# Score rectangles copied by ScalarE at block sizes 128 and 64 instead of masked copies by VectorE

## The chip, the cores and the metric

The kernel runs on one core of a Trainium2 chip. The metric is the device time of one execution in microseconds. A kernel's time is the median of several executions.

## The reference

One inference step of a two-layer decoder: 512 prompt tokens and 64 sample tokens (eight sequences of eight), width 1024. Each layer projects the normalised tokens, runs four recurrent mixers (HGRN2, GLA, RWKV-7, retention), merges them through gates, and ends with a SwiGLU feed-forward part. The change lies in the mixer core that HGRN2 and GLA share. Its scores decay with the distance of the two tokens:

```python
b = jnp.cumsum(gb, axis=2)
diff = b[:, :, :, None, :] - b[:, :, None, :, :]
decay = jnp.exp(jnp.where(causal > 0, diff, 0.0)) * causal
scores = jnp.sum(qb[:, :, :, None, :] * kb[:, :, None, :, :] * decay, axis=-1)
o = (jnp.einsum('bhts,bhsv->bhtv', scores, vb)
     + jnp.einsum('bhtk,bhkv->bhtv', qb * jnp.exp(b), S))
```

A score counts only when its key token is not later than its query token. The diagonal (a token with itself) has decay 1.

## The kernel before

`gla_core` works on chunks of 128 tokens, four for the prompt, and one of 64 for the samples. It runs once for HGRN2 (`nt` = 2, two tiles of channels) and once for GLA (`nt` = 1) in each layer, so there are 16 prompt chunks in all. Scores of a chunk are made level by level: at level m (64, 32, 16, 8, 4, 2, 1) the chunk is cut into blocks of 2m tokens, and the keys of a block's first half meet the queries of its second half. `gla_level` prepares a level: VectorE subtracts the decay sum at the middle of the block (L1107, tile `le`), ScalarE takes two exponentials of it (L1110), VectorE (HGRN2) or GpSimd (GLA) makes the scaled keys `lk` (L1111), and VectorE the scaled queries `qt` or `qg` (L1122, L1115). TensorE then multiplies them (L1026, tile `lvp` in PSUM), and `gla_pred` puts the wanted part of that product into the score tile `sc` by one `copy_predicated` on VectorE with an integer mask `lev` (L1137). The mask of a level also takes the diagonal score of each block's first query token (position m of the block). The diagonal positions that no level takes, one in 128 prompt tokens and one in 8 sample tokens, stand in a short list: `gd0` (GpSimd, L980 and L981) holds q times k there, a matmul sums it over a head's channels (`gdp`, L986 and L988), VectorE multiplies by v (`gdv`, L992 and L993) and adds it to the outputs at the end (L1092 and L1093).

The loop over levels prepares level i+1, then calls `gla_pred` for level i-1, then yields, then issues the matmul of level i. The `lvp` tiles and most other PSUM tiles of the mixers share a ring of two buffers (`g`). The masks, `sc` and the padded query tiles are allocated once.

The mixers are Python generators that are advanced between the projection units (`mix`, L1623), by a table of start and due positions (`PACE`). A projection unit is a matmul series (`pb<-h,whl`, L241 to L243) whose weights come by DMA into `raw`, are split into two float16 parts by ScalarE (L228) and VectorE (L229), and whose result ScalarE moves out of PSUM (L487 and others). The tile framework then orders the instructions of each engine itself, starting from the order of the text. Each engine runs its own list in order.

Other work that matters below: the RWKV mixer's VectorE and ScalarE parts (lines 577 to 965), and `head_rms_out` (L515 and L516, tile `hsq`), whose logarithm and exponential each come with a load of ScalarE's function table.

Of the kernel before, what the change touches and what calls it, by code (L numbers as in the profile page):

```python
# [16 lines left out]
ADD, SUB, MUL, MAX, MIN = ALU.add, ALU.subtract, ALU.mult, ALU.max, ALU.min  # L17

D = 1024
SEQ = 512  # L20
NS = 64
T = SEQ + NS
# [152 lines left out]
class Net:  # L175
# [792 lines left out]
    def gla_core(self, l, q, k, v, lg, nt, load, result):  # L968
# [3 lines left out]
        nc = self.nc  # L972
        hpt = 4 // nt
        dk = 128 // hpt
        B = lg
        d0 = self.t("gq", [128, nt, 12], "gd0")
        for j in range(nt):
            self.chunk_sums(B[:, j], lg[:, j], "ones")

            nc.gpsimd.tensor_tensor(d0[:, j, 0:4], q[:, j, 0:SEQ:128], k[:, j, 0:SEQ:128], op=MUL)  # L980
            nc.gpsimd.tensor_tensor(d0[:, j, 4:12], q[:, j, SEQ:T:8], k[:, j, SEQ:T:8], op=MUL)  # L981
            yield
        dp = self.psum("g", [128, 2, 12], "gdp")
        for j in range(2):
            if nt == 2:
                nc.tensor.matmul(dp[:, j], self.cf("head"), d0[:, j], start=True, stop=True)  # L986
            else:
                nc.tensor.matmul(dp[:, j], self.cf("gla_head")[:, 128 * j:128 * j + 128], d0[:, 0],  # L988
                                 start=True, stop=True)
        dv = self.t("gq", [128, 2, 12], "gdv")  # L990
        for j in range(2):
            nc.vector.tensor_tensor(dv[:, j, 0:4], dp[:, j, 0:4], v[j][:, 0:SEQ:128], op=MUL)  # L992
            nc.vector.tensor_tensor(dv[:, j, 4:12], dp[:, j, 4:12], v[j][:, SEQ:T:8], op=MUL)  # L993
        O = [self.t("gs", [128, T], "gl_o") for _ in range(2)]
        vw = 256 // nt
        S = None
        for c in range(5):
            samp = c == 4
            n = 64 if samp else 128
            ts = slice(128 * c, 128 * c + n)  # L1000
            if samp:
                sst = load(0)
                sc = self.scs
            else:
                sc = self.sc[self.nsc % 2]
# [3 lines left out]
            if nt == 1:  # L1009

                qm = self.qm[c % 2][:, :, :n]
                for h in range(4):
                    r = slice(32 * h, 32 * h + 32)
# [3 lines left out]
            for i, (li, m) in enumerate(lv):  # L1017
# [6 lines left out]
                ps = self.psum("g", [128, 4, 64], f"lvp{nt}")  # L1024
# [15 lines left out]
            if samp:  # L1040
                qz = self.padded(nt)
                for h in range(hpt):
                    r = slice(dk * h, dk * h + dk)
# [45 lines left out]
        if nt == 1:  # L1089
            nc.sync.dma_start(out=self.io["sample_gla"][l].rearrange("b h k v -> (h k) b v"), in_=so)  # L1090
        for j in range(2):
            nc.vector.tensor_tensor(O[j][:, 0:SEQ:128], O[j][:, 0:SEQ:128], dv[:, j, 0:4], op=ADD)  # L1092
            nc.vector.tensor_tensor(O[j][:, SEQ:T:8], O[j][:, SEQ:T:8], dv[:, j, 4:12], op=ADD)  # L1093
        result += [O, S]
        yield

# [35 lines left out]

    def gla_pred(self, sc, ps, li, m, n):

        so = sc[:n, :, :n].rearrange("p h (b u i) -> p h b u i", u=2, i=m)[:, :, :, 1]
        mk = self.lev[:n, li, None, :n // 2].to_broadcast([n, 4, n // 2])
        self.nc.vector.copy_predicated(so, mk.rearrange("p h (b i) -> p h b i", i=m),  # L1137
                                       ps[:n, :, :n // 2].rearrange("p h (b i) -> p h b i", i=m))
# [815 lines left out]
```

## Time and profile before

| | us |
|---|---|
| median of 3 runs (2200.36 to 2207.76) | 2204.15 |
| the profiled execution, its own time | 2207.72 |
| its span from the first to the last instruction | 2205.9 |
| TensorE busy with matmuls | 2039.1 |
| VectorE busy | 1636.6 |
| ScalarE busy | 1081.3 |
| GpSimd busy | 682.3 |

PE is TensorE's matmuls, PEld its weight loads, DVE VectorE, ACT ScalarE, POOL GpSimd. A busy TensorE isn't TensorE at its peak, since matmuls overlap and their ends are modelled. The mixers of the first layer lie between about 56 and 420 us, those of the second about 1080 us later. HGRN2's prompt chunks are worked on from 68 to 175 us, GLA's from 180 to 325 us.

### The profile page before, as it was taken

The numbers are of one execution on the slowest core, as the hardware profiler recorded it, in microseconds if no ns is written. First come the engines' busy times: TensorE is split into PE (matmuls) and PEld (weight loads), VectorE is DVE, ScalarE is ACT, GpSimd is POOL, SyncE is SP. The second block draws the span as 40 slices with busy tenths as digits, with TensorE's granted clock in tenths as the row PEclk, the third lists the DMA queues.
The fourth block names the chain that finished last, engine by engine and source line by source line (L and its number), as shares of the span: only waits on it lengthen the run. The fifth ranks groups of instructions, "written<-read, shape, count | busy, mean of one in ns | idle before, by whom it ended". The sixth has DMA issues, their size and how long they took to land.

```text
span 2205.9 us, 42236 instructions
## 1 busy us (share of the span) xinstructions
PE 2039.1 (92%) x15754; PEld 1612.3 (73%) x15754; DVE 1636.6 (74%) x3409; ACT 1081.3 (49%) x2524; POOL 682.3 (31%) x889
## 2 busy tenths in 40 slices
PE   7989999998888899999999889989998988999998
PEld 5767787786676677777777778768776766777776
DVE  7889667768785899863488986586788779998441
ACT  6554546345444555442466355453645465554332
POOL 2223222146550544320012142213465316443000
PEclk9999999999999999999999999999999999999999
DMA  6312224333435344343421222242343443443331
GB/s 181 84 41 62 58 58 110 77 83 92 116 98 177 80 116 120 87 135 103 122 68 46 58 62 60 73 111 62 87 120 88 131 141 97 111 116 87 121 106 51
DMA packets 373498, 209.59 MB, mean 95 GB/s; under 512 B 59810, under 2 KB 360410, under 8 KB 373292
## 3 DMA queue, kind: packets, MB, share of 16 engines
q1 hardware_dynamic: 365516, 192.73, 31.6%
q0 software_dynamic: 7776, 14.16, 3.6%
q8 instruction: 124, 2.03, 0.4%
q14 instruction: 82, 0.67, 0.1%
HBM read 173.72 MB, written 16.59 MB: 86 GB/s over the span
## 4 chain that ended last, share of the span: by engine, by line
PE 47%; DVE 28%; ACT 8%; issue 7%; DMA 5%; POOL 3%; SPq 1%; DVEq 0%; ACTq 0%; POOLq 0%
PE pb L243 5%; PE pb L242 5%; PE pb L241 5%; PE xb L243 4%; PE xb L242 4%; PE xb L241 4%; DVE hA L1704 4%; DVE hS L1704 3%; DVE sc L1745 2%; DVE fy L1776 2%; DVE whl L229 2%; DVE su L1745 2%; PE fsS L1731 2%; PE fsS L1729 2%; PE fsS L1730 2%
## 5 line engine op out<-in xcount | busy, mean ns | idle before, releaser
L241 PE MATMUL pb<-h,whl 128*128 128x288 f16 (+1 forms) x1504 | 435.8, 290 | 4.4 <-ACT h L464 2.2
L243 PE MATMUL pb<-h,whl 128*128 128x288 f16 (+1 forms) x1504 | 435.5, 290 | 3.2 <-DVE whl L229 3.1
L242 PE MATMUL pb<-h,whl 128*128 128x288 f16 (+1 forms) x1504 | 436.0, 290 | 0.6 <-DVE h L465 0.4
L229 DVE SCALAR_TENSOR_TENSOR whl<-raw,whl 128x512 f16<-128x512 f32 (+1 forms) x352 | 253.8, 730 | 134.3 <-ACT whl L228 132.2
L242 PEld LDWEIGHTS <-whl 128*128 128x128 f16 (+1 forms) x2784 | 275.4, 99 | 88.0 <-issue 13.5
L243 PEld LDWEIGHTS <-whl 128*128 128x128 f16 (+1 forms) x2784 | 275.1, 99 | 88.0 <-issue 12.7
L241 PEld LDWEIGHTS <-whl 128*128 128x128 f16 (+1 forms) x2784 | 277.2, 100 | 76.6 <-issue 3.6
L228 ACT ACTIVATE whl<-raw 128x512 f16<-128x512 f32 (+1 forms) x352 | 213.3, 618 | 168.2 <-PE pb L243 51.9
L243 PE MATMUL xb<-fa,whl 128*128 128x288 f16 x704 | 201.3, 286 | 0.0
L242 PE MATMUL xb<-fa,whl 128*128 128x288 f16 x704 | 201.3, 286 | 0.0
L241 PE MATMUL xb<-fa,whl 128*128 128x288 f16 x704 | 201.3, 286 | 0.0
L1729 PE MATMUL fsA<-h,hA 128*128 128x288 f16 x432 | 124.3, 288 | 14.9 <-DVE gu L1550 10.8
L1729 PE MATMUL fsS<-st,hS 128*128 128x288 f16 x456 | 132.6, 291 | 5.9 <-ACT hS L1703 5.9
L1731 PE MATMUL fsS<-st,hS 128*128 128x288 f16 x456 | 132.4, 290 | 0.4 <-DVE hS L1704 0.3
L1730 PE MATMUL fsS<-st,hS 128*128 128x288 f16 x456 | 132.5, 291 | 0.0
L1731 PE MATMUL fsA<-h,hA 128*128 128x288 f16 x432 | 124.2, 288 | 1.7 <-DVE hA L1704 1.6
L1730 PE MATMUL fsA<-h,hA 128*128 128x288 f16 x432 | 124.3, 288 | 0.0
L1707 POOL TENSOR_TENSOR raw<-raw 128x512 f32<-128x512 f32 x52 | 79.0, 1520 | 134.2 <-DVE hA L1704 129.7
L1729 PEld LDWEIGHTS <-hS 128*128 128x128 f16 x864 | 85.7, 99 | 35.9 <-ACT hS L1703 13.7
L1704 DVE SCALAR_TENSOR_TENSOR hA<-sraw,hA 128x512 f16<-128x512 f32 x110 | 103.1, 945 | 10.6 <-ACT hA L1703 10.6
L1707 POOL TENSOR_TENSOR sraw<-sraw 128x512 f32<-128x512 f32 x60 | 89.7, 1499 | 51.4 <-DVE hA L1704 45.7
L1731 PEld LDWEIGHTS <-hS 128*128 128x128 f16 x864 | 85.7, 99 | 24.8 <-DVE hS L1704 2.6
(486 smaller groups left out, 5257.8 us busy)
## 6 DMA issues: line engine op xcount, KB each, us to landing
raw<-in_w_in SPq DMA_DIRECT2D x208, 256.0 KB
sraw<-in_w_ffn_in SPq DMA_DIRECT2D x40, 512.0 KB
raw<-in_w_ffn_out SPq DMA_DIRECT2D x80, 256.0 KB
raw<-in_w_ffn_in SPq DMA_DIRECT2D x78, 256.0 KB
x<-xd SPq DMA_DIRECT2D x32, 288.0 KB
raw<-sraw POOLq DMA_DIRECT2D x34, 256.0 KB, 3.3
sraw<-in_w_in SPq DMA_DIRECT2D x32, 256.0 KB
raw<-in_w_out SPq DMA_DIRECT2D x32, 256.0 KB
```

The source lines that it names most:

```text
L228: nc.scalar.activation(hl[:, 0, :n], raw[:, :n], AF.Copy, scale=WS)
L229: nc.vector.scalar_tensor_tensor(hl[:, 1, :n], raw[:, :n], WS, hl[:, 0, :n], op0=MUL, op1=SUB)
L241: nc.tensor.matmul(ps, wh, hi, start=i == 0, stop=False)
L242: nc.tensor.matmul(ps, wh, lo, start=False, stop=False)
L243: nc.tensor.matmul(ps, wl, hi, start=False, stop=i == len(ks) - 1)
L1704: nc.vector.scalar_tensor_tensor(hl[:, 1], a, WS, hl[:, 0], op0=MUL, op1=SUB)
L1707: nc.gpsimd.tensor_tensor(dst, a, b, op=op)
L1729: nc.tensor.matmul(ps, w[a][:, 0, k], hi, start=k == 0, stop=False)
L1730: nc.tensor.matmul(ps, w[a][:, 0, k], lo, start=False, stop=False)
L1731: nc.tensor.matmul(ps, w[a][:, 1, k], hi, start=False, stop=k == 3)
L1745: nc.vector.tensor_tensor(o, a, p, op=ADD)
L1776: nc.vector.scalar_tensor_tensor(y, u, PH * AS, sg, op0=MUL, op1=MUL)
```

## The change

The two coarsest levels of a prompt chunk (m = 64 and m = 32) no longer use the mask. For each block, ScalarE copies the rectangle of keys of the first half by queries of the second half from PSUM to `sc`: one copy of 64 partitions by 4 heads by 64 columns at m = 64, and two copies of 32 partitions by 4 heads by 32 columns at m = 32. The rectangle has no diagonal element, so the list of diagonal scores takes every 32nd prompt token in place of every 128th: 16 prompt entries and 8 sample entries instead of 4 and 8. Levels 16 to 1 and the sample chunk stay as they are.

```diff
-        d0 = self.t("gq", [128, nt, 12], "gd0")
+        d0 = self.t("gq", [128, nt, 24], "gd0")
...
-            nc.gpsimd.tensor_tensor(d0[:, j, 0:4], q[:, j, 0:SEQ:128], k[:, j, 0:SEQ:128], op=MUL)
-            nc.gpsimd.tensor_tensor(d0[:, j, 4:12], q[:, j, SEQ:T:8], k[:, j, SEQ:T:8], op=MUL)
+            nc.gpsimd.tensor_tensor(d0[:, j, 0:16], q[:, j, 0:SEQ:32], k[:, j, 0:SEQ:32], op=MUL)
+            nc.gpsimd.tensor_tensor(d0[:, j, 16:24], q[:, j, SEQ:T:8], k[:, j, SEQ:T:8], op=MUL)
...
-        dp = self.psum("g", [128, 2, 12], "gdp")
+        dp = self.psum("g", [128, 2, 24], "gdp")
...
-        dv = self.t("gq", [128, 2, 12], "gdv")
+        dv = self.t("gq", [128, 2, 24], "gdv")
         for j in range(2):
-            nc.vector.tensor_tensor(dv[:, j, 0:4], dp[:, j, 0:4], v[j][:, 0:SEQ:128], op=MUL)
-            nc.vector.tensor_tensor(dv[:, j, 4:12], dp[:, j, 4:12], v[j][:, SEQ:T:8], op=MUL)
+            nc.vector.tensor_tensor(dv[:, j, 0:16], dp[:, j, 0:16], v[j][:, 0:SEQ:32], op=MUL)
+            nc.vector.tensor_tensor(dv[:, j, 16:24], dp[:, j, 16:24], v[j][:, SEQ:T:8], op=MUL)
...
-            nc.vector.tensor_tensor(O[j][:, 0:SEQ:128], O[j][:, 0:SEQ:128], dv[:, j, 0:4], op=ADD)
-            nc.vector.tensor_tensor(O[j][:, SEQ:T:8], O[j][:, SEQ:T:8], dv[:, j, 4:12], op=ADD)
+            nc.vector.tensor_tensor(O[j][:, 0:SEQ:32], O[j][:, 0:SEQ:32], dv[:, j, 0:16], op=ADD)
+            nc.vector.tensor_tensor(O[j][:, SEQ:T:8], O[j][:, SEQ:T:8], dv[:, j, 16:24], op=ADD)
...
     def gla_pred(self, sc, ps, li, m, n):
 
+        if m >= 32:
+            for b in range(n // (2 * m)):
+                r = slice(2 * m * b, 2 * m * b + m)
+                self.nc.scalar.copy(sc[r, :, r.stop:r.stop + m], ps[r, :, m * b:m * b + m])
+            return
```

## Rows read from the trace of the kernel before

**Rows 1.** The page's first part: busy us, share of the span, instructions.
```profile
PE 2039.1 (92%) x15754; PEld 1612.3 (73%) x15754; DVE 1636.6 (74%) x3409; ACT 1081.3 (49%) x2524; POOL 682.3 (31%) x889
```

**Rows 2.** The page's chain that ended last, shares by engine.
```profile
PE 47%; DVE 28%; ACT 8%; issue 7%; DMA 5%; POOL 3%; SPq 1%; DVEq 0%; ACTq 0%; POOLq 0%
```

**Rows 3.** Busy time by stretch: stretch, length, PE, PEld, DVE, ACT, POOL, clock, DMA.
```profile
110.00:165.00 55.00, 47.24 (x334) 37.00 (x333) 48.62 (x114) 29.68 (x72) 12.05 (x20) 0.91 0.16 40
165.00:215.00 50.00, 46.59 (x350) 36.52 (x349) 45.80 (x141) 21.16 (x72) 17.90 (x35) 1.00 0.27 65
...
260.00:345.00 85.00, 84.07 (x666) 69.43 (x664) 51.88 (x146) 35.96 (x119) 23.12 (x50) 1.00 0.23 61
```

**Rows 4.** TensorE's timeline: start, length; in brackets the idle time before, and releaser.
```profile
102.75 0.68 PE L1026 MATMUL lvp<-qt,lk 128*128 128x128 f32 x4 [0.48 <-DVE qt L1122]
133.41 1.19 PE L1026 MATMUL lvp<-qt,lk 128*128 128x128 f32 x4 [3.50 <-DVE qt L1122]
...
184.56 0.42 PE L1026 MATMUL lvp<-qt,lk 128*64 128x64 f32 x4 [0.36 <-DVE qt L1122]
190.73 0.42 PE L1026 MATMUL lvp<-qt,lk 128*64 128x64 f32 x4 [0.58 <-DVE qt L1122]
...
225.41 1.19 PE L1026 MATMUL lvp<-qg,lk 128*128 128x256 f32 x2 [2.64 <-ACT hsq L515]
...
1304.98 0.67 PE L1026 MATMUL lvp<-qg,lk 128*128 128x256 f32 x2 [2.64 <-ACT hsq L515]
```

**Rows 5.** The masked copies of line 1137: durations in ns, and their waits.
```profile
L1137 DVE COPY_PREDICATED sc<-lev,lvp x112: 416/435/739, 69.2 to 1393.5; 128x256 f32<-128x256 int32 x112
...
  PE lvp L1026: 13.2, 19
```

**Rows 6.** VectorE's timeline around masked copies of the two coarse levels.
```profile
93.59 0.43 DVE L1137 COPY_PREDICATED sc<-lev,lvp 128x256 f32<-128x256 int32 x1
93.92 0.68 DVE L577 TENSOR_TENSOR rw_r<-cur 128x511 f32<-128x511 f32 x1
...
128.71 0.44 DVE L1137 COPY_PREDICATED sc<-lev,lvp 128x256 f32<-128x256 int32 x1
...
132.15 0.51 DVE L1111 TENSOR_TENSOR lk<-hg_k,le 128x256 f32<-128x256 f32 x1
...
182.84 0.43 DVE L1137 COPY_PREDICATED sc<-lev,lvp 128x256 f32<-128x256 int32 x1
...
186.17 0.43 DVE L1137 COPY_PREDICATED sc<-lev,lvp 128x256 f32<-128x256 int32 x1
```

**Rows 7.** ScalarE's copies out of PSUM into tile gkh, by form, durations in ns.
```profile
L1155 ACT COPY gkh<-gtp x24: 266/372/373, 84.9 to 1519.0; 128x256 f32<-128x256 f32 x16, 128x128 f32<-128x128 f32 x8
...
L1165 ACT COPY gkh<-gtp x8: 256/258/263, 196.8 to 1533.5; 64x128 f32<-64x128 f32 x8
```

**Rows 8.** ScalarE's timeline in HGRN2's third chunk.
```profile
117.85 1.28 ACT L1110 ACT_TABLE_LOAD   x1
119.14 0.31 ACT L1110 ACTIVATE le<-le 128x128 f32<-128x128 f32 x1
119.36 0.67 ACT L695 ACTIVATE rn<-rn 128x576 f32<-128x576 f32 x1
119.93 0.29 ACT L1110 ACTIVATE le<-le 128x128 f32<-128x128 f32 x1
...
131.27 0.51 ACT L1110 ACTIVATE le<-le 128x128 f32<-128x128 f32 x2
```

**Rows 9.** Busy time and granted clock behind three of TensorE's waits (columns as above).
```profile
133.50:137.00 3.50, 3.50 (x17) 2.59 (x18) 3.46 (x10) 1.45 (x6) 0.38 (x1) 0.55 0.47 122
225.40:229.00 3.60, 3.60 (x14) 2.34 (x15) 1.61 (x3) 3.10 (x6) 0.34 (x1) 0.53 0.24 54
1305.00:1309.00 4.00, 4.00 (x32) 3.35 (x33) 2.04 (x4) 3.36 (x7) 0.77 (x1) 1.00 0.23 52
```

**Rows 10.** GpSimd's products of the diagonal list in GLA, durations in ns.
```profile
L980 POOL TENSOR_TENSOR gd<-gl_q,gl_k x2: 259/259/259, 170.7 to 1250.2; 128x4 f32<-128x4 f32 x2
```

## The prediction

> **What bounds the kernel now.** I read the page's busy shares first: TensorE 92%, VectorE 74%, ScalarE 49% [rows 1]. By these alone VectorE would be cover for everything. The chain of waits says otherwise: 28% of it is VectorE and 8% ScalarE [rows 2]. So the next question is where VectorE sets the pace, and that a table by stretch answers. From 110 to 165 us VectorE is busy 48.62 of 55 us and TensorE 47.24; from 165 to 215 us VectorE is busy 45.80 of 50. From 260 to 345 us, where most of GLA's chunks run, TensorE is busy 84.07 of 85 us and VectorE 51.88 [rows 3]. So the same masked copy can be worth something in HGRN2's part and nothing in GLA's.
>
> What a shorter VectorE list can give back is only time in which TensorE stands still behind VectorE. TensorE's timeline gives these waits one by one. Those behind `qt` that bear on the change are 0.48 us at 102.75, 3.50 at 133.41, 0.36 at 184.56 and 0.58 at 190.73; one of 2.64 at 225.41 stands behind ScalarE's `hsq`. The second layer repeats the pattern about 1080 us later: the same 2.64 at 1304.98 [rows 4]. I therefore work out one layer and double it.
>
> **What is removed.** 16 prompt chunks with two coarse levels each lose 32 of the 112 full-size masked copies [rows 5]. Their length is bimodal: median 435 ns, longest 739 [rows 5]; the five coarser levels stand at 0.43 in the timeline, as at 93.59 and 128.71 [rows 6], so 32 x 0.435 = 13.9 us of VectorE's busy time go. On VectorE's list each takes less than its length, since the next instruction starts before it ends: 93.59 to 93.92 is 0.33 us [rows 6]. I use 0.33 for what a removed copy gives back where VectorE is the bound. A copy that itself waited for TensorE gives nothing; masked copies waited 19 times, 13.2 us in all [rows 5].
>
> Place by place, in the first layer:
>
> HGRN2, first chunk: TensorE has no wait behind it. 0.
>
> HGRN2, second chunk: the copy at 93.59 has a full VectorE list behind it up to the `qt` that releases TensorE at 102.75. Of the 0.48 us there, 0.33 go: -0.33 [rows 4, 6].
>
> HGRN2, third chunk: the copy at 128.71 stands ahead of the 3.50 us wait, in a VectorE stretch without gaps [rows 4, 6]. It looks like the best place, but `lk` at 132.15 also needs the two exponentials that begin at 131.27 and take 0.51, thus end at 131.78 [rows 6, 8]. That is 0.37 us of slack on ScalarE. The two new copies of m = 32 come ahead of these exponentials and take about 0.32 together (2 x 0.258 less the overlaps, below), so ScalarE's slack is used up just as VectorE would come 0.33 earlier. I take 0; the ends are -0.33 (the copies are placed behind) and +0.32 (they also delay the function table's load before it).
>
> HGRN2, fourth chunk: its two copies are among those that waited for TensorE [rows 5]. 0; a full VectorE list there would make it -0.66.
>
> GLA, first chunk: it runs while HGRN2's sample chunk keeps VectorE full (45.80 of 50 us [rows 3]). Its copies at 182.84 and 186.17 precede the `qt` of 184.56 and 190.73, with waits of 0.36 and 0.58: -0.33 each [rows 4, 6].
>
> GLA, second chunk: here the change costs. The wait of 2.64 us at 225.41 stands behind a stretch of ScalarE with its table loads [rows 4]. The copy of m = 64 now joins that list.
>
> GLA, third and fourth chunk: TensorE has 0.93 us idle in 85 [rows 3]; VectorE's gain and ScalarE's cost are both covered by matmuls. 0. If TensorE were not the bound there, these 4 copies would give 1.3 us per layer.
>
> **What is added.** Per chunk one ScalarE copy of 64 x 256 and two of 32 x 128. No row has these partitions, but 64 x 128 took 258 ns and 128 x 256 372 [rows 7], so I price by columns: 0.372 + 2 x 0.258 = 0.888 us, times 16 is 14.2 us of ScalarE. ScalarE's list also overlaps: an exponential of 0.31 begins at 119.14 and the next instruction at 119.36 [rows 8], 0.09 before its end. So the m = 64 copy costs the list 0.28 and each m = 32 copy 0.17. In the second GLA chunk this is +0.28 on TensorE's wait. Bounds for one copy: 0, since ScalarE is idle half the time [rows 1], and its full length.
>
> A copy now waits on ScalarE for its matmul, in place of the masked copy on VectorE. Queued behind it are the exponentials of later levels, the weight splits and the PSUM moves of the projections, and VectorE's `lk` and TensorE's next series wait for these. `gla_pred` runs one step after its matmul was issued, so mostly the product is there.
>
> The list of diagonals grows from 12 to 24 columns. On GpSimd the 128 x 4 product took 259 ns [rows 10]; at most four times that for 16 entries, 1.04 us, six times: 6 x 0.78 = 4.7 us at most, on an engine busy 12.05 of 55 us [rows 3], and read only a matmul series later. On TensorE and VectorE it is 12 more elements in instructions whose price is nearly all start-up. 0; without GpSimd's idle time it would be those 4.7 us.
>
> **Sum.** Per layer -0.33 - 0.33 - 0.33 + 0.28 = -0.71, both layers -1.4 us. The profiled execution's own time is 2207.72 (span 2205.9 and 1.8 around it), so it would become 2206.3. Against the median of the runs, 2204.15, it is 2202.7. The bounds of the parts, if everything lay on the path: -13.9 (2190.2) and +14.2 (2218.4).
>
> **A clock that follows the waits.** Behind the 3.50 us wait the granted clock was 0.55 for 3.5 us, mostly the 1.2 GHz level; behind the 2.64 us wait it was 0.53 in the first layer and 1.00 in the second [rows 9]. A drop costs about (1 - 0.55) x 3.5 = 1.6 or (1 - 0.53) x 3.6 = 1.7 us. So 0.3 us on a wait near this length can cost or save 1.7 more, once per place. The Trainium skill (TensorE: Matmul & The Clock Gate, "HAM oscillation") says that TensorE's clock is halved behind long idle stretches, so such a wait is paid twice. These rows agree in one layer and not in the other. By that rule the drop would come in both layers when the 2.64 grows, and the sum would be 2204.4. I give a second drop at this place a quarter of the first case's chance below, 0.13; it stays inside that case's own range.
>
> **Rivals.** (a) Faster: VectorE's list is the real bound wherever HGRN2 is active, and its lateness is carried from wait to wait. Then the eight copies of HGRN2 and the two of GLA's first chunk count with their whole length: 20 x 0.435 = 8.7 us, 2195.5. For it: VectorE busy 48.62 of 55 and 45.80 of 50 [rows 3]. Against it: several of these copies waited for TensorE themselves, so VectorE was early there. The Trainium skill (Perfetto Trace Analysis, "Optimizing Scalar/DVE Operations") says that work may be moved to ScalarE where VectorE is saturated; the rows show it nearly saturated in these two stretches alone.
>
> (b) Slower: ScalarE's list becomes the wait. Each of the 48 copies, 0.296 us on average (14.2 / 48), stands in order ahead of exponentials for which VectorE waits. It decides from 22 copies on the path (22 x 0.296 = 6.5 us); with half of them, 24, it is +7.1, 2211.3. For it: the third chunk has ScalarE 0.37 us from being the bound. Against it: ScalarE is busy 29.68 of 55 and 21.16 of 50 us [rows 3].
>
> (c) The order changes. The two exponentials of one level, adjacent in the text, have line 695 between them [rows 8], so the framework orders the lists itself, and other instructions can move with this edit. A further pair of function table loads in each layer, or one fewer, is 2 x 2 x 1.28 = 5.1 us [rows 8]: 2209.3 or 2199.0.
>
> (d) The masked copies weren't on the path at all: 2204.15, within the first case's own range.
>
> **How the numbers follow.** About 0.3% (6.6 us) is what a measurement of this kernel can tell from no change. The sum's case, with (d), has 0.52. Its own range is 2199.6 to 2207.0: downwards four copies per layer at 0.35 (2.8) and a clock drop less (1.7); upwards 0.28 + 0.32 per layer (1.2) and a drop more (1.7). Case (a) has 0.22, (b) 0.14, (c) 0.12, half to each side and both within 0.3%. So faster 0.22, same 0.64, slower 0.14. The range runs from 2194.5, just past (a), to 2210.0, past (c) and short of (b); it leaves out about 0.1 on either side. The predicted time is 2202.7.
>
> **What would show it.** Line 1137 with 80 full-size copies, the long ones of 0.7 us all still there; VectorE's busy time down 13.9 to about 1622.7, ScalarE's up 14.2 to about 1095.5, with copies `sc<-lvp` near 0.37 and 0.26 us. TensorE's wait near 102.75 down to 0.15, those near 184.56 and 190.73 nearly gone, that at 225.41 up to about 2.9, the 3.50 unchanged. The prediction is wrong if the waits of 3.50 us, or those behind RWKV's parts, move by microseconds; if ScalarE's rows between 115 and 131 us or from 218 to 227 us stand in another order; or if waits appear on ScalarE behind `lvp`.

## The result, and the profile after

The changed kernel takes 2215.21 us (median of four executions, 2214.44 to 2217.91) against 2204.97 for the kernel before in the same comparison: a ratio of 1.0051 (1.0031 to 1.0070). Run again, in another comparison and with five executions, it was 1.0064 (1.0052 to 1.0076). It is slower by 10 to 14 us, where 2202.7 was predicted and 2210.0 was the upper end of the range. The profiled execution took 2214.49 us, its span 2212.7, 6.8 more than before.

The first part of the page after (busy us, share, instructions), which answers to [rows 1]:

```profile
PE 2047.9 (93%) x15754; PEld 1616.6 (73%) x15754; DVE 1622.7 (73%) x3377; ACT 1097.7 (50%) x2576; POOL 678.9 (31%) x889
```

VectorE's busy time fell by 13.9 us, to the tenth as the prediction said. ScalarE's rose by 16.4, not by 14.2. The view of the masked copies' line and of the new copies' line after (durations min/median/max in ns, then what the new copies waited for and who waited for them, us and times):

```profile
L1142 DVE COPY_PREDICATED sc<-lev,lvp x80: 417/434/736, 73.6 to 1402.3; 128x256 f32<-128x256 int32 x80
...
L1138 ACT COPY sc<-lvp x48: 238/257/366, 69.7 to 1384.2; 32x128 f32<-32x128 f32 x32, 64x256 f32<-64x256 f32 x16
...
  PE lvp L1026: 1.3, 3
who waited for it (us, times):
...
  PE hps L514: 2.4, 2
```

The copies are as long as [rows 7] made them, and they wait for their product three times only. But somebody waits for them: the matmul of `hps` (L514), twice, which is no reader of `sc`. And ScalarE's groups after hold something that isn't a copy (busy us, mean ns):

```profile
L515 ACT ACT_TABLE_LOAD x14 | 18.0, 1283 | 1.3 <-PE hps L514 1.1
...
L516 ACT ACT_TABLE_LOAD x8 | 10.3, 1283 | 0.1
```

Before, these two lines had 12 and 6 loads of the function table. Four more at 1.283 are 5.1 us of ScalarE. They stand in GLA's second chunk in both layers. ScalarE's timeline there, first layer, after:

```profile
221.18 1.28 ACT L516 ACT_TABLE_LOAD   x1
222.48 0.68 ACT L516 ACTIVATE hsq<-hsq 128x576 f32<-128x576 f32 x1
223.07 0.35 ACT L1138 COPY sc<-lvp 64x256 f32<-64x256 f32 x1
223.32 0.25 ACT L1110 ACTIVATE le<-le 128x64 f32<-128x64 f32 x1
223.59 1.28 ACT L515 ACT_TABLE_LOAD   x1
224.89 0.50 ACT L515 ACTIVATE hsq<-hps,eps 128x288 f32<-128x288 f32 x1
225.41 1.28 ACT L1110 ACT_TABLE_LOAD   x1
226.70 0.26 ACT L1110 ACTIVATE le<-le 128x64 f32<-128x64 f32 x1
226.97 1.28 ACT L515 ACT_TABLE_LOAD   x1
228.27 0.50 ACT L515 ACTIVATE hsq<-hps,eps 128x288 f32<-128x288 f32 x1
228.67 0.24 ACT L1138 COPY sc<-lvp 32x128 f32<-32x128 f32 x1
228.92 1.28 ACT L516 ACT_TABLE_LOAD   x1
230.22 0.68 ACT L516 ACTIVATE hsq<-hsq 128x576 f32<-128x576 f32 x1
```

The same place in the kernel before:

```profile
223.47 1.28 ACT L515 ACT_TABLE_LOAD   x1
224.76 0.89 ACT L515 ACTIVATE hsq<-hps,eps 128x288 f32<-128x288 f32 x2
225.67 1.28 ACT L1110 ACT_TABLE_LOAD   x1
...
227.13 0.67 ACT L516 ACTIVATE hsq<-hsq 128x576 f32<-128x576 f32 x1
```

Before, the two logarithms of L515 stand side by side behind one table load, and L516 comes at 227.13. After, an exponential of `le` stands between them, the table is loaded for L515, L1110, L515 and L516 in turn, and L516 comes at 230.22, 3.1 us later. TensorE's timeline after shows what stands behind the parting of the logarithms, and what follows in the second layer (in brackets the idle time before, and releaser):

```profile
221.51 0.65 PE L514 MATMUL hps<-hsq,cst 128*128 128x288 f32 x2
...
223.47 0.75 PE L514 MATMUL hps<-hsq,cst 128*128 128x288 f32 x2 [1.18 <-ACT sc L1138]
225.49 1.19 PE L1026 MATMUL lvp<-qg,lk 128*128 128x256 f32 x2 [1.26 <-issue]
...
1317.74 2.08 PE L950 MATMUL ixp<-itt,imu 128*128 128x128 f32 x8 [3.84 <-DVE itt L946]
```

The tile `hps` is made in two halves, and both come from the ring `g`, the one of two buffers that `lvp` uses. Before, the two halves ran without a wait, and VectorE's masked copy at 221.27 let the buffer of the `lvp` of m = 64 go:

```profile
221.51 1.13 PE L514 MATMUL hps<-hsq,cst 128*128 128x288 f32 x4
...
221.27 0.44 DVE L1137 COPY_PREDICATED sc<-lev,lvp 128x256 f32<-128x256 int32 x1
```

After, the second half waits for that buffer. ScalarE lets it go, in order behind the table load of L516 and L516 itself, at 223.42. So the input of the second logarithm comes later than that of the first, and in this kernel's list the framework has put an exponential between them. VectorE's timeline in the second layer, after, shows the delay going on:

```profile
1309.12 0.43 DVE L1115 TENSOR_TENSOR qg<-qm,le 128x256 f32<-128x256 f32 x1 [2.19 <-ACT le L1110]
...
1313.07 0.82 DVE L521 SCALAR_TENSOR_TENSOR gl_o<-gl_o,pc,hsq 128x576 f32<-128x576 f32 x1 [3.06 <-ACT hsq L516]
...
1316.98 0.70 DVE L946 STREAM_TRANSPOSE itt<-iw 128x512 f32<-128x512 f32 x1
```

and the same part before:

```profile
1307.40 0.82 DVE L521 SCALAR_TENSOR_TENSOR gl_o<-gl_o,pc,hsq 128x576 f32<-128x576 f32 x1 [1.28 <-ACT hsq L516]
...
1311.67 0.70 DVE L946 STREAM_TRANSPOSE itt<-iw 128x512 f32<-128x512 f32 x1
```

VectorE idles 2.19 and 3.06 us there (the two waits in these places were 0.98 and 1.28 before). RWKV's transpose `itt` comes 5.3 us later; of these, 2.6 had been lost ahead of this place (the `hps` before this one begins at 1299.07, where it began at 1296.45 before), so the place itself adds 2.7. TensorE waits 3.84 us for `itt` (1.17 before). In the first layer of the same profile that wait is 0.84 us and no half clock follows it, so the table loads come in both layers and the long wait behind them only in one.

In HGRN2's part TensorE's timeline after, with the rows that answer to [rows 4]:

```profile
131.35 0.30 PE L241 MATMUL pb<-h,whl 128*128 128x288 f16 x1 [0.24 <-ACT whl L228]
...
132.68 0.30 PE L243 MATMUL pb<-h,whl 128*128 128x288 f16 x1 [0.91 <-DVE whl L229]
...
134.86 0.68 PE L1026 MATMUL lvp<-qt,lk 128*128 128x128 f32 x4 [1.64 <-DVE qt L1122]
...
145.70 0.71 PE L1056 MATMUL gop<-sc,vz 128*128 128x128 f32 x4 [0.92 <-DVE vz L1157]
...
155.56 0.68 PE L1026 MATMUL lvp<-qt,lk 128*128 128x128 f32 x4 [3.88 <-DVE qt L1122]
...
183.24 0.42 PE L1026 MATMUL lvp<-qt,lk 128*64 128x64 f32 x4 [0.15 <-DVE qt L1122]
...
189.41 0.42 PE L1026 MATMUL lvp<-qt,lk 128*64 128x64 f32 x4 [0.71 <-DVE qt L1122]
...
195.40 1.07 PE L1056 MATMUL gop<-scs,vz 64*128 64x64 f32 x8 [1.28 <-DVE sc L1142]
```

The 3.50 us wait of the third chunk has split into 0.24, 0.91 and 1.64, and 0.92 stands at 145.70 (0.32 before). The last row is new: `gop` of the sample chunk waits 1.28 us for a masked copy of GLA's first chunk (in the second layer 1.29). Before, the nearest wait was 1.01 at 195.12, for `gl_kh`. The granted clock behind this wait and behind that of 3.84 us, after (length, busy times, clock in the third column from the right):

```profile
197.00:200.40 3.40, 3.40 (x19) 2.57 (x19) 2.41 (x9) 0.65 (x3) 2.81 (x9) 0.58 0.44 106
...
1317.80:1324.60 6.80, 6.80 (x31) 5.46 (x32) 4.15 (x9) 1.10 (x3) 4.13 (x11) 0.55 0.31 77
```

Both stretches are mostly at the 1.2 GHz level, as the first two of [rows 9]. The Trainium skill (TensorE: Matmul & The Clock Gate, "HAM oscillation") says that behind a long wait TensorE's clock is halved, so that the wait is paid a second time. The row behind the wait of 3.84 us agrees. The wait of 1.28 us is shorter than those that the section speaks of; for it the row above stands alone.

### The profile page after: what moved, and what is told of

Read it like the earlier page. It is cut to its first block, busy times and chain, and to the rows that moved or that the text cites. A ratio compares the mean times of both kernels' runs of the same rounds, so it can differ in the third digit from the quotient of the medians.

```text
span 2212.7 us, 42265 instructions
## 1 busy us (share of the span) xinstructions
PE 2047.9 (93%) x15754; PEld 1616.6 (73%) x15754; DVE 1622.7 (73%) x3377; ACT 1097.7 (50%) x2576; POOL 678.9 (31%) x889
## 4 chain that ended last, share of the span: by engine, by line
PE 48%; DVE 26%; ACT 9%; issue 7%; DMA 4%; POOL 4%; SPq 0%; DVEq 0%; ACTq 0%; POOLq 0%
PE pb L241 4%; PE pb L243 4%; PE pb L242 4%; PE xb L243 4%; PE xb L242 4%; PE xb L241 4%; DVE hA L1709 3%; DVE hS L1709 2%; PE fsS L1736 2%; PE fsS L1734 2%; PE fsS L1735 2%; DVE sc L1750 2%; DVE fy L1781 2%; DVE whl L229 2%; DVE su L1750 2%
```

## The experiments

T1 says that the loss lies in one copy per layer, that of m = 64 in GLA's second chunk, by the late buffer of the ring `g` and the extra table loads. T1b, added after the first four runs, says that HGRN2's part of the loss is the wait at `gop` and the half clock behind it. T2 is the prediction's rival (b): the copies cost because they stand in ScalarE's list, wherever they are.

Each run was compared with executions of the kernel before that were taken beside it; the runs fall into four such comparisons, and two ratios from different comparisons are set against each other only through the kernel before. Each execution has a span and a mean granted clock. The span times (1 - clock) is an estimate of the time lost to the clock, as if TensorE had work in all of the time at the lower clock; the remainder is then what the lists themselves take. The last two columns give both as means over all executions, minus those of the kernel before in the same comparison. Their standard errors are 1.1 to 2.7 us for the clock and 0.8 to 1.9 us for the rest, so single entries say little.

| run | copies on ScalarE | median, us | ratio to before (95%) | clock | rest |
|---|---|---|---|---|---|
| changed again | 48 | 2218.07 | 1.0064 (1.0052 to 1.0076) | +10.3 | +3.7 |
| one back | 46 | 2210.98 | 1.0020 (1.0008 to 1.0032) | +5.4 | -0.2 |
| order fixed | 48 | 2210.28 | 1.0016 (1.0003 to 1.0028) | +6.3 | -2.6 |
| HGRN2 only | 24 | 2208.23 | 1.0018 (1.0007 to 1.0029) | +4.5 | -0.7 |
| GLA only | 24 | 2213.58 | 1.0034 (1.0023 to 1.0045) | +3.9 | +4.4 |
| list only | 0 | 2208.22 | 1.0002 (0.9989 to 1.0016) | +2.4 | -1.2 |
| all on VectorE | 0 | 2208.34 | 1.0005 (0.9993 to 1.0016) | -2.4 | +3.6 |
| gop elsewhere | 48 | 2209.22 | 1.0014 (1.0002 to 1.0026) | -0.8 | +4.0 |
| before, gop elsewhere | none | 2207.91 | 1.0007 (0.9997 to 1.0018) | +0.8 | +1.2 |
| one forward | 2 | 2215.28 | 1.0045 (1.0032 to 1.0057) | +6.4 | +3.3 |
| both mended | 48 | 2212.61 | 1.0031 (1.0020 to 1.0043) | +6.2 | +0.7 |
| HGRN2, all chunks | 24 | 2205.82 | 1.0007 (0.9997 to 1.0016) | +1.0 | +0.6 |
| HGRN2, first three | 18 | 2203.91 | 0.9997 (0.9987 to 1.0006) | +2.0 | -2.7 |
| HGRN2, middle two | 12 | 2202.59 | 0.9995 (0.9982 to 1.0007) | -0.5 | -0.8 |
| the same again | 12 | 2203.37 | 0.9997 (0.9987 to 1.0008) | +1.5 | -2.1 |
| HGRN2, third | 6 | 2202.29 | 0.9994 (0.9984 to 1.0004) | 0.0 | -1.5 |

**One copy back to VectorE.** In `gla_pred`, with `dve` true for `nt == 1 and c == 1 and m == 64`:

```diff
-                self.nc.scalar.copy(sc[r, :, r.stop:r.stop + m], ps[r, :, m * b:m * b + m])
+                (self.nc.vector.tensor_copy if dve else self.nc.scalar.copy)(
+                    sc[r, :, r.stop:r.stop + m], ps[r, :, m * b:m * b + m])
```

> One rectangle per layer, that of m = 64 in GLA's second chunk, is copied by VectorE; the other 46 copies stay on ScalarE. T1 (late PSUM buffer): the two logarithms of that stretch stand together again, L515 has 12 function table loads and not 14, L516 6 and not 8; the 6.8 to 10 us come back: 2202 to 2207, ratio 0.998 to 1.001. T2 (ScalarE's list as a whole): two copies of 48 are gone, so at most 1 us comes back: 2213 to 2216.

ScalarE's groups (as above):

```profile
L515 ACT ACT_TABLE_LOAD x12 | 15.4, 1283 | 1.3 <-PE hps L514 1.1
...
L516 ACT ACT_TABLE_LOAD x6 | 7.7, 1283 | 0.1
```

The loads are those of before, as T1 said, and the ratio falls from 1.0064 to 1.0020: 0.0044, or 9.7 us, for 2 of 48 copies. T2 allowed 1 us. (Against the first ratio of the changed kernel, 1.0051, it is 6.8 us.) But T1 had expected everything back, and 0.2% stays.

**One copy forward.** The reverse: the same line, with VectorE making all rectangles but those two.

> All rectangles are copied by VectorE except one per layer, that of m = 64 in GLA's second chunk, which ScalarE copies: 2 of 48 copies. The kernel with all 48 on VectorE was level with before (1.0005). T1: this one copy alone brings the late PSUM buffer (1.18 us wait at hps), the two extra pairs of table loads on L515 and L516 and what follows: 1.002 to 1.004, 2210 to 2215. T2: two copies of 0.37 us, at most 0.7 us: 1.000 to 1.001, 2205 to 2209.

TensorE's timeline in the first layer:

```profile
223.36 0.75 PE L514 MATMUL hps<-hsq,cst 128*128 128x288 f32 x2 [1.18 <-ACT sc L1138]
...
234.23 2.08 PE L950 MATMUL ixp<-itt,imu 128*128 128x128 f32 x8 [2.58 <-DVE itt L946]
```

All of it is there: the late buffer, 14 and 8 table loads, the late `itt`, and half clock behind that (`ixp` takes 2.08 us; in the kernel before it took 1.16 at 1312.43). The wait for `itt` is 2.58 us in both layers. The ratio is 1.0045, a little above T1's range, against 1.0005 with all copies on VectorE: 0.0040 or 8.8 us for two copies of 0.35 us. This and the run before show T1's place in both directions, and T2 falls as an account of GLA's part.

**The order fixed.** An ordering edge and no wait: GLA's exponentials that stand behind HGRN2's second logarithm (`ln`) in the text stay behind it in ScalarE's list.

```diff
+                if name == "hg" and j == 1:
+                    self.ln = ln
...
-            nc.scalar.activation(e, e, AF.Exp, scale=sign)
+            ex = nc.scalar.activation(e, e, AF.Exp, scale=sign)
+            if nt == 1 and getattr(self, "ln", None) is not None:
+                self.tc.add_manual_dep(ex.ins, self.ln.ins.name, mybir.DependencyInfo(
+                    mybir.DependencyClass.NoSync, mybir.DependencyReason.DATA), reason="order")
```

> The changed kernel with all copies on ScalarE; only the order is fixed: in GLA's second chunk no exponential stands between the two logarithms of HGRN2's output norm. The copy of m = 64 still stands behind the function table load, so the PSUM buffer is still late. T1: the two extra pairs of table loads go, 5.1 us and what follows from them; the late buffer stays (TensorE's wait of 1.2 us at the tile hps): 2205 to 2210. T2: 2213 to 2216.

ScalarE's timeline, and TensorE's:

```profile
225.94 0.35 ACT L1143 COPY sc<-lvp 64x256 f32<-64x256 f32 x1
...
227.60 0.89 ACT L515 ACTIVATE hsq<-hps,eps 128x288 f32<-128x288 f32 x2
...
226.34 0.75 PE L514 MATMUL hps<-hsq,cst 128*128 128x288 f32 x2 [1.18 <-ACT sc L1143]
```

The copy is still late and TensorE still waits 1.18 us at `hps`, but the logarithms are side by side and the 1.0064 falls to 1.0016, as low as with the copy back on VectorE. So the late buffer by itself costs nothing that these runs can tell: the price is that of the reordering that goes with it in the changed kernel.

**One mixer alone.** Rectangles and long list for `nt == 2` only, or for `nt == 1` only. The score tiles are shared, so in both kernels they keep diagonal values that the other mixer's masks wrote, and some scores are not the reference's; all instructions are there.

> The rectangles and the long list in HGRN2 alone; GLA keeps masks and the short list. T1: no extra table loads, HGRN2's places give what little they give: 2200 to 2206. T2: half of the copies, half of the loss: 2208 to 2211.

> The rectangles and the long list in GLA alone; HGRN2 keeps masks and the short list. T1: the whole loss, with the extra table loads: 2212 to 2218. T2: half of the copies, half of the loss: 2208 to 2211.

GLA alone is 1.0034, HGRN2 alone 1.0018: together 0.0052, the loss of the changed kernel in its first comparison. Neither theory had foreseen this split: GLA's time fell into T1's range and HGRN2's into T2's. GLA's part is T1's. HGRN2's 4.0 us has no further table load in it, and by the table it is mostly clock (+4.5, rest -0.7). This kernel has the wait of 1.30 us at `gop`, and its windows show the clock behind it in both layers:

```profile
200.00:203.40 3.40, 3.40 (x17) 2.17 (x17) 2.51 (x8) 0.41 (x1) 3.00 (x9) 0.51 0.45 114
1278.50:1282.00 3.50, 3.50 (x17) 2.22 (x17) 2.51 (x8) 0.41 (x1) 2.94 (x9) 0.53 0.53 133
```

That is (1 - 0.51) x 3.40 + (1 - 0.53) x 3.50 = 3.3 us, and T1b was formed from it.

**The list alone, and all on VectorE.** The first takes the diagonal out of the masks of m = 64 and 32 (`& (m < 32)`) and keeps the masked copies. The second replaces `scalar.copy` by `vector.tensor_copy`.

> The masked copies of all levels stay on VectorE (the masks of m = 64 and 32 without their diagonal), and only the list of diagonal scores grows to 24 columns; ScalarE gets no copy. T1b, formed from the four runs before: the part of the loss that HGRN2 alone shows (1.0018) comes from another order of TensorE's list at the end of HGRN2's sample chunk, where gop then waits 1.3 us and the clock falls to half for 3.4 us, in both layers; this order stands in this kernel too, so 2208 to 2211, with the wait at gop near 195 and 1275 us. T2 (ScalarE's copies): no copy, no loss: 2204 to 2207.

> The same rectangles and list, but all 48 copies are made by VectorE. T1 and T1b: the PSUM buffer ahead of hps comes free in time, 12 table loads on L515, no loss in GLA; the order at HGRN2's gop is that of the changed kernel, so its wait and its half clock stay: 2207 to 2211. T2: no copy on ScalarE, 2204 to 2207, or above that only if VectorE's 48 copies take more than the 32 masked ones.

Both are level with before; their times lie in T1b's ranges only because the kernel before took 2206.28 beside them. T1b had expected 4 us more with the list alone, and that is wrong: the order came as expected, but the wait was shorter.

```profile
196.51 1.07 PE L1056 MATMUL gop<-scs,vz 64*128 64x64 f32 x8 [1.13 <-DVE sc L1137]
```

No half clock follows it, in either layer. So the order at `gop` can come without the copies on ScalarE, and in these profiles half clock follows only the longer wait. With all rectangles on VectorE T1b's wait did not come at all: `gop` waits 0.22 us, `gtp` ahead of it 1.13, without half clock.

**Another ring for gop.** In the changed kernel and in the kernel before:

```diff
-            ops = self.psum("g", [128, 2, 128], "gop")
+            ops = self.psum("b" if samp and nt == 2 else "g", [128, 2, 128], "gop")
```

> The changed kernel with all copies on ScalarE; the PSUM tile gop of HGRN2's sample chunk is taken from the projections' ring of buffers instead of the mixers' ring of two. T1 and T1b: gop no longer waits for a masked copy of GLA's first chunk, so the half clock near 197 and 1277 us goes; the ring's turns shift by one, and with them the late slot at hps: 12 table loads on L515. 2200 to 2206. T2: the 48 copies stay on ScalarE, so the loss stays: 2210 to 2216.

> The kernel before with that one tile from the projections' ring: what the ring alone is worth. In its trace gop did not wait, but gtp just before it did for 1.0 us, without half clock. T1b: 0 to 2 us faster, 2203 to 2207. If it gains as much as the run with rectangles does against the changed kernel, the ring says nothing of the change.

With the changed kernel the half clock near 197 and 1277 us is gone, L515 has 12 loads, and the ratio falls to 1.0014. But `hps` still waits 1.18 us for `sc` in both layers, against the expectation, and 0.14% stays:

```profile
225.37 0.75 PE L514 MATMUL hps<-hsq,cst 128*128 128x288 f32 x2 [1.18 <-ACT sc L1138]
...
226.79 0.89 ACT L515 ACTIVATE hsq<-hps,eps 128x288 f32<-128x288 f32 x2
```

Here the logarithms stand side by side behind the late buffer, with no ordering edge. So a late buffer doesn't by itself part them; what made the framework choose was not found. The kernel before gains nothing by the other ring (1.0007, where T1b had expected 0 to 2 us less).

**Both mended.** The order fixed, and `gop` from the other ring.

> All 48 copies stay on ScalarE; both places are mended: no exponential between the two logarithms in GLA's second chunk, and gop of HGRN2's sample chunk from the projections' ring. T1 and T1b: what is left is the late slot at hps (1.2 us in each layer) against the small gains in HGRN2: 2203 to 2208. T2: 2211 to 2216.

A miss for T1 and T1b: 1.0031, with 63 table loads as before and no half clock at `gop`. It is above either mending alone, though the intervals meet, and the time lies in T2's range. The clock is lost elsewhere (+6.2); where was not found.

**HGRN2 chunk by chunk.** VectorE makes all rectangles except those of the chunks named; in the line of the first experiment the choice is `nt == 2`, `nt == 2 and c < 3`, `nt == 2 and c in (1, 2)` or `nt == 2 and c == 2`.

> ScalarE copies the rectangles of all four HGRN2 chunks (12 copies per layer), VectorE all others. T1b: in TensorE's list gop of the sample chunk stands as in the changed kernel: it waits 1.2 to 1.3 us and half clock follows near 200 and 1280 us: 1.0010 to 1.0020. T2, each copy costs: 1.0015 to 1.0020.

> The same without the fourth chunk (9 copies per layer). T1b: gop stands as in the kernel with the two middle chunks, waits about 0.5 us, and no half clock follows: 0.998 to 1.0005. T2, each copy costs: three quarters of the run before, 1.0011 to 1.0015.

> ScalarE copies the rectangles of HGRN2's second and third chunk alone (6 copies per layer); VectorE copies all others. A try for a kernel that beats both. T1b: the 3.50 us wait of the third chunk splits into 0.9 and 1.6 as in the other kernels with ScalarE's copies there (0.95 us less in each layer), no extra table loads, and if the 0.9 us wait for vz at the end of that chunk and the 1.3 us at gop do not come, 2202 to 2205; if they come, 2206 to 2210. T2: 12 copies of 48, a quarter of the loss: 2208 to 2210.

> The kernel with the second and third chunk once more, for a closer ratio than 0.9995 (0.9982 to 1.0007). T1b: 0.998 to 1.000. T2: 1.0007 to 1.001.

> ScalarE copies the rectangles of HGRN2's third chunk alone (3 copies per layer), VectorE all others. T1b: the wait of 3.5 us there splits as before and gop waits about 0.5 us: 0.998 to 1.0005. T2: a quarter of HGRN2's loss, 1.0003 to 1.0006.

All are level with before, and none is measurably faster. `gop` waits 0.47 us with the two middle chunks, and 0.48 with the first three or the third alone:

```profile
194.94 1.10 PE L1056 MATMUL gop<-scs,vz 64*128 64x64 f32 x8 [0.47 <-DVE sc L1143]
```

With all four chunks `gop` waited 0.22 us and not 1.2, as had been expected; `gtp` just ahead of it waited 1.13 us, without half clock. So the 24 copies on ScalarE that cost 4.0 us with GLA's masks cost 1.5 us here, within the uncertainty of nothing. T2 had wanted 1.0015 to 1.0020 there, which the interval just reaches, and at least 1.0011 with the first three chunks, which it doesn't (1.0006 at most). That speaks against T2 in HGRN2 too. In all five, the 3.50 us wait has become 0.2, 0.9 and 1.64, together 0.7 less. Behind it 0.6 to 0.85 us are given back, at the 0.7 to 0.9 us for `vz` (0.32 before) and the 3.88 to 3.90 us ahead of the next `lvp` (3.64 before).

**The changed kernel again.**

> The changed kernel itself once more, in the same call as the next three, for a closer ratio than four executions give. All theories: 1.004 to 1.006, 2213 to 2218. T1b: half clock near 198 and 1280 us in its trace, behind waits of 1.3 us at gop, as in the other four kernels with that wait or the profile of the changed kernel.

The waits of 1.29 and 1.28 us at `gop` are there again, with half clock behind them.

## Why the prediction was wrong

**The step that failed** is "GLA, second chunk": +0.28 per layer for the copy of m = 64 that joins ScalarE's list. It measured 3.4 to 4.9 per layer (both layers: 8.8 forward; 9.7 back against the second ratio of the changed kernel, 6.8 against the first). The place was right, the mechanism was not. I priced the copy as time in the list of the engine that makes it, and looked for who waits for `sc`. The bill came from what the copy lets go: a buffer of the ring `g` that `hps` needs next. The masked copy on VectorE had let it go at 221.27, the copy on ScalarE stands behind a function table load and lets it go at 223.42. Had I followed the buffer of that `lvp` to its next owner, I should have found that the second half of `hps` comes late, and with it the input of the second logarithm. That the framework then parts the two logarithms, which is what costs, doesn't follow from this alone: with `gop` elsewhere it did not. The wait itself went another way than the 2.9 us that was forecast at 225.41: it became 1.18 at `hps` and 1.26 at `lvp`, and the loss came behind it.

**Rival (c)** named the mechanism's outward sign, a further pair of table loads in each layer, gave it 0.06 on the slow side, and priced it at 5.1 us. Both were too small. The loads are exactly the four that it counted, but behind them VectorE idles, RWKV's `itt` is late, and TensorE waits for it. In the four kernels with parted logarithms (the changed one twice, GLA only, one forward) that wait was 2.16 to 3.84 us in six of eight places, with half clock behind it, and 0.84 and 0.86 us in the other two, without. How much of it is list and how much clock isn't settled: forward, against all on VectorE, the table has +8.8 clock and -0.3 rest; back, between the changed kernel run again and the one without this copy, 4.9 and 3.9. The prediction's separate price of a clock drop (1.6 to 1.7 us) was right for the stretches of 3.4 and 3.5 us behind `gop` (1.4 to 1.7); the one of 6.8 us behind `itt` costs (1 - 0.55) x 6.8 = 3.1. The prediction had no drop for either place.

**The sign to watch** was in the last part: ScalarE's rows between 218 and 227 us in another order. That is what came, and so did the other sign, a wait behind RWKV's parts that moves by microseconds (1.17 to 3.84) and the 3.50 that fell apart. Waits of ScalarE behind `lvp` did not (1.3 us in three).

**Second chunk of HGRN2**, -0.33: not seen. TensorE's 0.48 at 102.75 became 0.50, 0.49 and 0.77. **GLA's first chunk**, -0.66: 0.36 became 0.15 and 0.58 became 0.71, and the wait of 1.01 at `gtp` became 1.28 at `gop` with half clock behind. At both places TensorE's and VectorE's lists stand in another order than before, so waits moved instead of shrinking, and 0.33 us per removed copy was measured nowhere. **Third chunk**, 0 with the 3.50 unchanged: the zero holds as a sum, by luck, and the sentence doesn't hold. The wait fell by 0.71 (to 0.24, 0.91 and 1.64) and rose by 0.6 and 0.24 at the next two places (0.32 before at 145.56, and 3.64 before at 154.43), 0.13 more in all.

**Busy times and durations** were right: the masked copies' 13.9 us, the ScalarE copies at 0.25 and 0.35 us, 13.7 in all. They decided nothing. **Rival (b)**, every copy on ScalarE's list, falls as an account of the whole: HGRN2's 24 copies cost 0.18% in one kernel and 0.07% in another, 18 and 12 cost nothing, while 2 in the wrong place cost 0.40%. Its number, 2211.3, is nearer to the measured time than the sum's, but for GLA's part the reason is another. **Rival (a)** found no support: VectorE's relief bought nothing that stayed.

What stays open is HGRN2's part. Alone it cost 0.18%, and that goes with the 1.3 us wait at `gop` and the half clock behind it: of the profiles here all five with that wait show the drop in both layers, and the other kernels, whose waits there are 1.14 us or less, show it once in 26 places (before with `gop` elsewhere, second layer). But four kernels with 46 or 48 copies on ScalarE and the logarithms side by side don't bear this out: with the half clock at `gop` they stand at 1.0016 (order fixed) and 1.0020 (one back), without it at 1.0014 (`gop` elsewhere) and 1.0031 (both mended). So that this wait is HGRN2's part was not shown, and the 0.14 to 0.31% that stays in all four has no shown cause. GLA's other 22 copies were not tried by themselves.

## What to carry to other kernels

When a reader of a PSUM tile moves to another engine, ask who gets the buffer next and when the new engine, in its own order, will let it go; that date can be worth more than the instruction's length by a factor of ten (here 4.4 us against 0.35). On an engine that switches function tables, look for two instructions of one table that stand side by side only because both inputs come in time: if one input is late, a foreign instruction can move between them and each switch is paid again. Where a framework makes the order of the lists, test a move in parts, since the cost can sit in 2 of 48 instructions.

## What the runs showed of the hardware

A function table load took 1.283 us each time, and the next function began 0.01 to 0.02 us behind it in 65 of the 67 cases after (in the other two it came 2.3 and 4.1 us later): 223.59 + 1.28 = 224.87, and the logarithm at 224.89. The Trainium skill (ScalarE: Activation LUTs, "What ACT_TABLE_LOAD costs") counts a drain of about 1.38 us on top for each switch. The rows above show none: ahead of that load the exponential ends at 223.32 + 0.25 = 223.57 and the load begins at 223.59, so a pair of switches here costs 2.6 us and not 5.3.

34 executions of the kernel before, in one comparison, ran from 2199.61 us at a granted clock of 0.980 to 2212.58 at 0.972: by the estimate above, the time lost to the clock is 44 us in the one and 62 in the other. The half-clock stretches come and go between executions of one program, and this spread is as large as the effect that was looked for. So a pair of profiles 6.8 us apart had to be read stretch by stretch.
